# Strassen-type up projection: activations made in two rounds, four products of the first two blocks regrouped, and one weight tile given its own buffer

## The chip, the cores and the metric

The kernel runs on one core of a Trainium2 chip. The metric is the device time of one execution in microseconds (us), the median of several runs. The engines that matter here are TensorE (PE in the profile: matrix products and transposes), VectorE (DVE: sums, differences, evictions), ScalarE (ACT: casts, copies, activations), GpSimd (POOL: a few sums and powers) and SyncE (SP), whose queue issues most of the transfers. Each engine works through its own list in a fixed order; semaphores make it wait for the others.

## The reference

One layer of a transformer over 1024 tokens of width 1024: a modulated norm, a token mixer (retention beside differential attention), an output projection with a gated residual, and then the part that this change touches:

```python
def conv_ffn(h, w_up, conv_w, conv_b, w_down):
    u = h @ w_up
    up = jnp.pad(u, ((0, 0), (1, 1), (0, 0)))
    u = up[:, :-2] * conv_w[0] + up[:, 1:-1] * conv_w[1] + up[:, 2:] * conv_w[2] + conv_b
    a, b = jnp.split(u, 2, axis=-1)
    return (jax.nn.silu(a) * b) @ w_down
...
    x = x + g1 * y_lat
    h2 = rms_norm(x, norm2_g[l]) * (1.0 + sc2) + sh2
    x = x + g2 * conv_ffn(h2, w_up[l], conv_w[l], conv_b[l], w_down[l])
```

`h` is 1024 x 1024, `w_up` is 1024 x 5632 and `w_down` 2816 x 1024; all is in 32-bit floats, and the final norm follows.

## The kernel before

**How a product is made.** Every 32-bit operand is split into a high and a low part (`split_op` for weights, `split_to` for activations: a cast on ACT, then a difference on DVE, lines 894 and 895, 941 and 942). A product then takes three matmuls per slice of 128 rows of the contraction: high by high, high by low, low by high (`passes`, lines 129 to 131). `product` does four slices, so 12 matmuls of 128x128 by 128x512.

**The up projection in blocks.** Block j holds 128 columns of the half `a` of `w_up` and the 128 matching ones of the half `b` (22 blocks). It is computed as a two by two matrix product in Winograd's form of Strassen's method, with 7 products (P1 to P7, 84 matmuls) in place of 8. The weights of a block come as two tiles `wra` and `wrb` of 512 KB, each with two buffers. Each tile holds two halves of the contraction: a1, a2, b1, b2. P1, P2 and P4 take a1, a2 and b2 as they are; P5, P6, P7 and P3 take sums made on POOL by `combined` (lines 1024 to 1027): s1 = b1 + b2, s2 = s1 - a1, s3 = a1 - b1 into `cmb` (three buffers), and a2 - s2 written over b1. The activations come as B11, B21 (first 512 tokens), B22 and the differences T1, T2, T3, T4: P1 uses B11, P2 B21, P3 B22, P4 T4, P5 T1, P6 T2, P7 T3.

**Banks.** P1, P6, P7 and P4 of a block add up in one PSUM bank, `chain`, which is copied out after each of them. P2 has the bank `second`. P5 and then P3 add up in the bank `third`, which is read once after P5 (into `ub`, line 1109) and once after P3 (into `ua`, line 1114). There are eight banks in pools of 4, 2 and 2.

**What surrounds the change.** The output projection ends with the norm of the eight token tiles (`norm2`). The first four tiles are turned beside it into B11 and B21 (`turned0`). The last four are turned by `turned1`, a generator of which `tick` runs a step every so many slices of a product (`beside(turned1(), 0.45, ...)`: 0.45 steps per slice): four rounds, each of which makes the difference for T1, then B22, T2, T3 and T4 for one slice, with 2 transposed groups on PE, 9 DVE and 7 ACT instructions. Beside it PE computes P1 and P2 of the first `NPRE` = 4 blocks, whose weights `pre` were loaded and for three blocks also split (`early`) during the output projection; the fourth split is made here. Then follow the sums of block 0 (`ops0`) and the loop over the blocks (line 1125): load of block j+1, `begin` (P1 and P2, unless done), `end` and `gated` of the block before (P3, P4, then convolution, silu, product and the operands for the down projection), and `middle` (P6, P5, P7).

**What sets the order.** Outside a part of the attention, the order of the instructions on each engine is not the one of the source. A planner puts them in order when the program is built, by the order of the source as priority and by its own estimates of when operands and buffers are ready. What it decided is fixed at run time: an instruction that waits holds up all behind it on its engine. Pools with `reuse_waits="tile"` wait for the tiles whose place they take, others for their whole predecessor.

The weights' split tiles `whi`, `wlo` rotate through six buffers (`wop`), so the split of one product can be made six products ahead of its use at most.

Of the kernel before, what the change touches and what calls it, by code (L numbers as in the profile page):

```python
# [8 lines left out]
F32 = mybir.dt.float32  # L9
# [63 lines left out]
def kernel(  # L73
# [78 lines left out]
    with ExitStack() as p1:  # L152
# [738 lines left out]
    def split_op(src):  # L891
        hi = wop.tile([P, 4, P], F32R, name="whi")
        lo = wop.tile([P, 4, P], F32R, name="wlo")
        nc.scalar.copy(hi, src)  # L894
        nc.vector.tensor_tensor(out=lo, in0=src, in1=r32(hi), op=ALU.subtract)  # L895
        return hi, lo

    def raw_load(name, src):
        o = wst.tile([P, KD, P], F32, name=name)
        nc.sync.dma_start(out=o, in_=src)  # L900
        return o

# [37 lines left out]
    def split_to(src, tt, c):  # L940
        nc.scalar.copy(tt[0][:, c, :], src)  # L941
        nc.vector.tensor_tensor(out=tt[1][:, c, :], in0=src, in1=r32(tt[0][:, c, :]), op=ALU.subtract)
# [4 lines left out]
            split_to(raw0[:, d, :], (B11, B21)[d // 4], d % 4)  # L947
            yield

    NPRE = 4  # L950
    with ExitStack() as p3:
        ps = p3.enter_context(tc.tile_pool(name="ps3", bufs=2, space=PSUM))
        for n in range(2):
            sl = wo_first if n == 0 else []
            for _ in wo_gen if n == 0 else out_weights(n, sl):
                pass
            for t in range(NT):
                pt = ps.tile([P, 512], F32, name="po3", tag="mm")
                for k in range(KD):
                    passes(pt, tuple(yT[a][t // 4][:, k, t % 4 * P : (t % 4 + 1) * P] for a in range(2)), sl[k], k == 0, k == KD - 1)  # L960
                    tick()
                dst = x1[t][:, n * 512 : (n + 1) * 512]
                gated = wo.tile([P, 512], F32, name="gated")
                nc.vector.tensor_tensor(out=gated, in0=pt, in1=g1[:, n * 512 : (n + 1) * 512], op=ALU.mult)
                nc.vector.tensor_tensor(out=dst, in0=gated, in1=dst, op=ALU.add)
                if n == 1:
                    norm2(t)
                    if t == 1:
                        pre = [raw_load("wra" if j < 2 else "wrb", w_up[j]) for j in range(NPRE)]
                        early = [[split_op(a[:, c : c + 4, :]) for c in (0, 4)] for a in pre[:3]]  # L970
                    if t == 3:
                        beside(turned0(), 0.5, -3.0)
        beside(iter(()), 0.0)
# [11 lines left out]
    def turned1():  # L985
        def less(o, a, b):
            nc.vector.tensor_tensor(out=o, in0=a, in1=b, op=ALU.subtract)

        for c in range(4):
            r12 = tmpT.tile([P, 512], F32, name="r12", bufs=2)  # L990
            turned(1, c, r12, True)
            b11, b21 = raw0[:, c, :], raw0[:, c + 4, :]
# [12 lines left out]
            yield  # L1005

    def up_load(j):
        return raw_load("wra", w_up[j]), raw_load("wrb", w_up[j + NF])
# [9 lines left out]

    def combined(j):

        a, b = raws.pop(0)
        a1, a2, b1, b2 = a[:, 0:4, :], a[:, 4:8, :], b[:, 0:4, :], b[:, 4:8, :]
        s1, s2, s3 = [cmb.tile([P, 4, P], F32, name="cmb", bufs=3) for _ in range(3)]
        nc.gpsimd.tensor_tensor(out=s1, in0=b1, in1=b2, op=ALU.add)  # L1024
        nc.gpsimd.tensor_tensor(out=s2, in0=s1, in1=a1, op=ALU.subtract)
# [4 lines left out]
    chain, second, first = {}, {}, {}  # L1030
# [12 lines left out]
    beside(iter(()), 0.0)  # L1043
    raws.append(up_load(1))
    pstS.close()
    tmpS.close()
    rawp.close()
    psC = ctx_r.enter_context(tc.tile_pool(name="psC", bufs=2, space=PSUM, side="right"))
    bank_cycle = itertools.cycle([psC] * 2 + [psB] * 2 + [psA] * 4)


    with ExitStack() as p4:
        up = p4.enter_context(tc.tile_pool(name="up", bufs=2, side="right", reuse_waits="tile"))

        def conv(u, idx):
# [4 lines left out]
            nc.vector.scalar_tensor_tensor(out=t[:, : L - 1], in0=u[:, 1:], scalar=w[2], in1=t[:, : L - 1], op0=ALU.mult, op1=ALU.add)  # L1060
            return t

        held = {}

        def down_operands(j, g):
# [17 lines left out]
        class Block:  # L1083
            def __init__(self, j):
                self.j = j
                self.ops = combined(j) if j else ops0

            def op(self, p):
                return split_op(self.ops[p])
# [10 lines left out]
                self.ub = up.tile([P, L], F32, name="ub")  # L1100

            def middle(self):
                product(self.chain, self.op("p6"), T2, False)
                nc.scalar.copy(self.ua[:, 512:], self.chain)
                self.third = bank("third")
                product(self.third, self.op("p5"), T1, True)
                product(self.chain, self.op("p7"), T3, False)
                nc.scalar.copy(self.ub[:, 512:], self.chain)
                nc.vector.tensor_tensor(out=self.ub[:, 512:], in0=self.third, in1=self.ub[:, 512:], op=ALU.add)

            def end(self):
                product(self.third, self.op("p3"), B22, False)
# [10 lines left out]

        last = None
        for j in range(NF):
            if 2 <= j + 1 < NF:
# [252 lines left out]
```

## Time and profile before

| | us |
|---|---|
| median of three runs | 1448.55 (1448.17 to 1450.31) |
| the profiled execution's own time | 1441.0 |
| its span, first to last instruction | 1439.2 |
| PE busy in the span | 1379.9 (96%) |
| DVE busy | 1003.8 (70%) |
| ACT busy | 732.4 (51%) |
| POOL busy | 340.8 (24%) |
| granted PE clock, mean | 0.992 |
| PE busy, 700 to 783.32 (output projection) | 83.32 of 83.32 |
| PE busy, 783.32 to 866.65 (first blocks) | 75.68 of 83.33 |
| PE busy, 870 to 1215 (further blocks) | 345.00 of 345.00 |

In the profile each instruction has a line number, an operation, and the tiles that it writes and reads; "idle before" is the time its engine stood still ahead of it, with the instruction that ended the wait. Matmuls are pipelined: their start to start distance, not their duration, is their cost on PE.

### The profile page before, as it was taken

Reading aid. Unit: us, or ns where it says so; the run is one execution under the profiler, and the core shown is the slowest. Engines: PE = TensorE matmul, PEld = TensorE weight load, DVE = VectorE, ACT = ScalarE, POOL = GpSimd, SP = SyncE. Lnnn points to the kernel's source line nnn. Section 1 sums busy time; section 2 is a strip of 40 time slices with the busy share of each in tenths; the row PEclk is TensorE's granted clock in tenths of the full one; section 3 lists DMA queues with packets and bytes.
Section 4 is the critical chain, followed back from the end, with each engine's and each line's share of the span. In section 5 each row is a group of like instructions: output and inputs, shape, how many; then the busy total and the mean of one; then the engine's idle time right before and its main releaser. Section 6 shows DMA issues by size and latency. Waiting matters only on the chain.

```text
span 1439.2 us, 19420 instructions
## 1 busy us (share of the span) xinstructions
PE 1379.9 (96%) x6924; PEld 1141.9 (79%) x6924; DVE 1003.8 (70%) x1493; ACT 732.4 (51%) x1394; POOL 340.8 (24%) x451
## 2 busy tenths in 40 slices
PE   6999999999899899999999899999999999999996
PEld 2678787887777789999888677888888888888885
DVE  3565655333677598888346888878777777998457
ACT  3535512322456688998224655555555545455533
POOL 1210000022787323431002253322223230000001
PEclk9999999999999999999999999999999999999999
DMA  8557655466455767480511123223222224953224
GB/s 332 199 194 240 219 196 190 137 193 195 134 173 164 208 156 164 121 143 1 220 62 78 59 104 118 108 110 110 92 87 93 110 110 174 391 206 102 101 95 176
DMA packets 107673, 218.30 MB, mean 152 GB/s; under 512 B 8948, under 2 KB 47348, under 8 KB 106680
## 3 DMA queue, kind: packets, MB, share of 16 engines
q1 hardware_dynamic: 99448, 192.14, 38.3%
q0 software_dynamic: 8128, 24.91, 7.7%
q8 instruction: 55, 0.90, 0.3%
q14 instruction: 42, 0.34, 0.1%
HBM read 159.61 MB, written 57.41 MB: 151 GB/s over the span
## 4 chain that ended last, share of the span: by engine, by line
PE 66%; DVE 8%; DMA 5%; POOL 3%; issue 3%; ACT 3%; SPq 0%; POOLq 0%; DVEq 0%; ACTq 0%
PE chain L129 5%; PE pv L760 5%; PE chain L130 5%; PE pA L728 5%; PE chain L131 5%; PE c L131 4%; PE c L129 4%; PE c L130 4%; PE third L130 2%; PE third L129 2%; PE third L131 2%; DMA W<-w_down 2%; PE pt L748 2%; PE pn L130 2%; PE pn L131 2%
## 5 line engine op out<-in xcount | busy, mean ns | idle before, releaser
L129 PE MATMUL chain<-T,whi 128*128 128x512 f32 x264 | 103.8, 394 | 4.9 <-ACT T L941 3.3
L129 PE MATMUL pl<-hT,whi 128*128 128x512 f32 x256 | 107.1, 419 | 0.0
L130 PE MATMUL chain<-T,whi 128*128 128x512 f32 x264 | 103.2, 391 | 0.0
L131 PE MATMUL chain<-T,wlo 128*128 128x512 f32 x264 | 102.6, 390 | 0.0
L131 PE MATMUL pl<-hT,wlo 128*128 128x512 f32 x256 | 100.5, 393 | 0.0
L130 PE MATMUL pl<-hT,whi 128*128 128x512 f32 x256 | 100.5, 393 | 0.0
L731 DVE TENSOR_REDUCE mt<-pA 128x1 f32<-128x1280 f32 x64 | 95.3, 1490 | 3.3 <-PE pA L728 1.5
L728 PE MATMUL pA<-ks,qhl 128*128 128x512 f32 (+1 forms) x384 | 91.6, 375 | 4.7 <-ACT p L735 4.7
L1024 POOL TENSOR_TENSOR cmb<-wrb 128x512 f32<-128x512 f32 x22 | 36.2, 1647 | 243.2 <-DMA wrb<-w_up 141.3
L131 PE MATMUL c<-whi,ghl 128*128 128x512 f32 x232 | 90.4, 390 | 0.2 <-DVE ghl L1183 0.2
L130 PE MATMUL c<-wlo,ghl 128*128 128x512 f32 x232 | 90.3, 389 | 0.0
L129 PE MATMUL c<-whi,ghl 128*128 128x512 f32 x232 | 90.2, 389 | 0.0
L115 POOL TENSOR_TENSOR sm<-sm,mhalf 128x1 f32<-128x1 f32 x26 | 16.1, 621 | 304.7 <-DVE sm L114 301.4
L735 ACT ACTIVATE p<-pA,mt 128x1280 f32<-128x1280 f32 x64 | 85.5, 1336 | 4.6 <-DVE mt L731 4.5
L894 ACT CAST whi<-cmb 128x512 fp32r<-128x512 f32 x66 | 41.0, 622 | 83.5 <-PE chain L130 63.7
L728 PEld LDWEIGHTS pA<-ks,qhl 128*128 128x128 f32 x384 | 68.9, 193 | 17.5 <-ACT p L735 5.8
L129 PE MATMUL pn<-whi,hT 128*128 128x512 f32 x192 | 79.1, 412 | 0.0
L760 PE MATMUL pv<-va,aT 128*128 128x128 f32 x640 | 77.0, 275 | 0.1
L131 PE MATMUL pn<-whi,hT 128*128 128x512 f32 x192 | 75.9, 398 | 0.5 <-DVE hT L540 0.5
L130 PE MATMUL pn<-wlo,hT 128*128 128x512 f32 x192 | 76.1, 396 | 0.0
L895 DVE TENSOR_TENSOR wlo<-cmb,whi 128x512 fp32r<-128x512 f32 x66 | 60.7, 922 | 20.2 <-ACT whi L894 20.2
L760 PEld LDWEIGHTS pv<-va,aT 128*128 128x128 f32 x640 | 74.0, 192 | 0.7 <-DVE yT L789 0.3
(301 smaller groups left out, 3884.1 us busy)
## 6 DMA issues: line engine op xcount, KB each, us to landing
wm<-w_mod SPq DMA_DIRECT2D x32, 512.0 KB, 4.4
raw<-w_in SPq DMA_DIRECT2D x28, 512.0 KB, 4.4
wra<-w_up SPq DMA_DIRECT2D x24, 512.0 KB, 3.2
wrb<-w_up SPq DMA_DIRECT2D x24, 512.0 KB, 3.5
W<-w_down SPq DMA_DIRECT2D x44, 256.0 KB, 6.4
ad<-s SPq DMA_DIRECT2D x20, 512.0 KB, 3.4
wra<-ad SPq DMA_DIRECT2D x20, 512.0 KB, 3.2
wrb<-ad SPq DMA_DIRECT2D x18, 512.0 KB, 3.3
```

The source lines that it names most:

```text
L115: nc.gpsimd.tensor_tensor(out=out_ap, in0=out_ap, in1=mhalf[:, :n], op=ALU.pow)
L129: mm(ps, lh, rh, start=first, stop=False, skip_group_check=more)
L130: mm(ps, lh, rl, start=False, stop=False, skip_group_check=more)
L131: mm(ps, ll, rh, start=False, stop=last, skip_group_check=more)
L728: mm(self.pa[m][:, c0:c1], self.q[:, i, m, qs], self.k[:, m, c0:c1], start=(i == 0), stop=(i == 1))
L731: nc.vector.tensor_reduce(out=self.mt[:, m : m + 1], in_=self.pa[m][:, :LK], axis=AX.X, op=ALU.min)
L735: nc.scalar.activation(self.p[m], self.pa[m][:, :LK], AF.Exp, scale=-1.0, bias=self.mt[:, m : m + 1], accum_out=self.s[:, m : m + 1])
L748: nc.tensor.transpose(self.pt[g][:, i, :], self.p[0][:, (4 * g + i) * P : (4 * g + i + 1) * P], ident)
L760: mm(self.pv, self.aT[:, c, :], self.v[:, c, :], start=(c == 0), stop=(c == NKT - 1))
L894: nc.scalar.copy(hi, src)
L895: nc.vector.tensor_tensor(out=lo, in0=src, in1=r32(hi), op=ALU.subtract)
L1024: nc.gpsimd.tensor_tensor(out=s1, in0=b1, in1=b2, op=ALU.add)
```

## The change

- **Loads.** `NPRE` goes from 4 to 3. The freed buffer of `wrb` and the next ones of `wra` take the weights of blocks 0 and 1 (`NSUM` = 2), all four tiles loaded during the output projection. The weights of block 2 are asked for at the start of the block loop, its b tile first, into a pool of its own (`third_b`), then its a tile, in this order on the queue. The loads of blocks 3 and later follow in the loop as before.
- **Sums.** For blocks 0 and 1 POOL makes three of the four sums in place, over the loaded tiles, during the output projection (`sums_in_place`); the fourth, s3 = b2 - a1, which is the same value, goes to `cmb` afterwards.
- **Two rounds.** `turned1` first makes T1, B22 and T3 for all four slices, with the value that T2 needs left in place in `raw0`; a second round of four steps makes T2 and T4. The rate is 0.36 steps per slice.
- **Products ahead.** P5 and P3 of blocks 0 and 1 are split and computed straight after P1 and P2 of the first three blocks, each in its own bank (`fifth`, `third`), ahead of P6. In these two blocks `middle` adds `fifth` to `ua` and to `ub`, `end` adds `third` to `ua`.

The core of the diff:

```diff
-    NPRE = 4
+    NPRE = 3
+    NSUM = 2
+    def up_load(j):
+        if j == NSUM:
+            start = len(nc.cur_bb.bb.instructions)
+            b = raw_load("wrb", w_up[j + NF], third_b)
+            a = raw_load("wra", w_up[j])
+            in_order(start)
+            return a, b
+        return raw_load("wra", w_up[j]), raw_load("wrb", w_up[j + NF])
+
+    def sums_in_place(a, b):
+        a1, a2, b1, b2 = a[:, 0:4, :], a[:, 4:8, :], b[:, 0:4, :], b[:, 4:8, :]
+        nc.gpsimd.tensor_tensor(out=b1, in0=b1, in1=b2, op=ALU.add)
+        nc.gpsimd.tensor_tensor(out=a1, in0=b1, in1=a1, op=ALU.subtract)
+        nc.gpsimd.tensor_tensor(out=a2, in0=a2, in1=a1, op=ALU.subtract)
...
+                        raws = [up_load(j) for j in range(NSUM)]
+                        for a, b in raws:
+                            sums_in_place(a, b)
...
-            less(r22, r22, b11)
-            split_to(r22, T2, c)
+            less(b11, r22, b11)
             split_to(r12, T3, c)
-            less(b21, b21, r22)
+            yield
+        for c in range(4):
+            b11, b21 = raw0[:, c, :], raw0[:, c + 4, :]
+            split_to(b11, T2, c)
+            less(b21, b21, b11)
             split_to(b21, T4, c)
             yield
...
+        if j < NSUM:
+            s3 = cmb.tile([P, 4, P], F32, name="cmb", bufs=3)
+            nc.gpsimd.tensor_tensor(out=s3, in0=b2, in1=a1, op=ALU.subtract)
+            return dict(p3=a2, p4=b2, p5=b1, p6=a1, p7=s3)
...
-    beside(turned1(), 0.45, 0.0)
+    ops = [combined(j) for j in range(NSUM)]
+    split_ahead = []
+    beside(turned1(), 0.36, 0.0)
     for j in range(NPRE):
-        if j == 3:
-            early.append([split_op(pre[j][:, c : c + 4, :]) for c in (0, 4)])
...
         if j < 2:
+            split_ahead += [split_op(ops[i][("p5", "p3")[j]]) for i in range(NSUM)]
             first[j] = first_sum(chain[j], second[j])
-    raws = [up_load(0)]
-    ops0 = combined(0)
+    pstS.close()
+    psC = ctx_r.enter_context(tc.tile_pool(name="psC", bufs=2, space=PSUM, side="right"))
+    for j, pool in enumerate((psA, psC)):
+        fifth[j] = bank("fifth", pool)
+        product(fifth[j], split_ahead[j], T1, True)
+    for j, pool in enumerate((psB, psC)):
+        third[j] = bank("third", pool)
+        product(third[j], split_ahead[NSUM + j], B22, True)
...
+        third_b = p4.enter_context(tc.tile_pool(name="third_b", bufs=1, side="right", reuse_waits="tile"))
+        raws.append(up_load(NSUM))
...
+                if j < NSUM:
+                    self.third, self.fifth = third[j], fifth[j]
+                    nc.vector.tensor_tensor(out=self.ua[:, 512:], in0=self.fifth, in1=self.ua[:, 512:], op=ALU.add)
+                else:
+                    self.third = self.fifth = bank("third")
+                    product(self.third, self.op("p5"), T1, True)
```

More of the change, by code (lines that the diff above doesn't have):

```diff
@@ L896, in split_op, with raw_load @@
         return hi, lo
-    def raw_load(name, src):
-        o = wst.tile([P, KD, P], F32, name=name)
+    def raw_load(name, src, pool=None):
+        o = (pool or wst).tile([P, KD, P], F32, name=name)
         nc.sync.dma_start(out=o, in_=src)
@@ L969 @@
                         pre = [raw_load("wra" if j < 2 else "wrb", w_up[j]) for j in range(NPRE)]
-                        early = [[split_op(a[:, c : c + 4, :]) for c in (0, 4)] for a in pre[:3]]
+                        early = [[split_op(a[:, c : c + 4, :]) for c in (0, 4)] for a in pre]
+                        raws = [up_load(j) for j in range(NSUM)]
+                        for a, b in raws:
+                            sums_in_place(a, b)
                     if t == 3:
@@ L1028, in combined @@
         return dict(p1=a1, p2=a2, p3=b1, p4=b2, p5=s1, p6=s2, p7=s3)
-    chain, second, first = {}, {}, {}
-    beside(turned1(), 0.45, 0.0)
+    chain, second, first, fifth, third = {}, {}, {}, {}, {}
+    ops = [combined(j) for j in range(NSUM)]
+    split_ahead = []
+    beside(turned1(), 0.36, 0.0)
     for j in range(NPRE):
-        if j == 3:
-            early.append([split_op(pre[j][:, c : c + 4, :]) for c in (0, 4)])
         chain[j] = bank("chain", psA)
@@ L1085, in __init__ @@
                 self.j = j
-                self.ops = combined(j) if j else ops0
+                self.ops = ops[j] if j < NSUM else combined(j)
             def op(self, p):
@@ L1102, in middle @@
             def middle(self):
+                j = self.j
                 product(self.chain, self.op("p6"), T2, False)
                 nc.scalar.copy(self.ua[:, 512:], self.chain)
-                self.third = bank("third")
-                product(self.third, self.op("p5"), T1, True)
+                if j < NSUM:
[4 more added lines that the diff above has]
+                    product(self.third, self.op("p5"), T1, True)
                 product(self.chain, self.op("p7"), T3, False)
                 nc.scalar.copy(self.ub[:, 512:], self.chain)
-                nc.vector.tensor_tensor(out=self.ub[:, 512:], in0=self.third, in1=self.ub[:, 512:], op=ALU.add)
+                nc.vector.tensor_tensor(out=self.ub[:, 512:], in0=self.fifth, in1=self.ub[:, 512:], op=ALU.add)
             def end(self):
-                product(self.third, self.op("p3"), B22, False)
+                if self.j >= NSUM:
+                    product(self.third, self.op("p3"), B22, False)
                 product(self.chain, self.op("p4"), T4, False)
@@ L1125 @@
         for j in range(NF):
-            if 2 <= j + 1 < NF:
+            if NSUM < j + 1 < NF:
                 raws.append(up_load(j + 1))
```

7 lines of the change are left out of this document (1 added, 6 removed).

## The prediction

> **What bounds the kernel now.** I read first the busy time by stage, then who waited for whom on PE where it isn't full, then PE's timeline around each wait, and last the chain that ended the longest one.
>
> ```profile
> core 0: us, PE busy (x) PEld busy (x) DVE busy (x) ACT busy (x) POOL busy (x), PEclk, DMA share, GB/s
> 700.00:783.32 83.32, 83.32 (x384) 68.99 (x383) 41.91 (x68) 23.83 (x39) 5.11 (x8) 1.00 0.33 127
> 783.32:866.65 83.33, 75.68 (x333) 59.49 (x331) 72.43 (x90) 48.54 (x77) 36.23 (x20) 0.98 0.23 85
> 870.00:1215.00 345.00, 345.00 (x1523) 285.50 (x1522) 275.49 (x311) 175.88 (x254) 93.60 (x69) 1.00 0.29 106
> 818.36:821.51 3.15, 3.15 (x7) 2.48 (x8) 3.15 (x4) 1.70 (x4) 1.65 (x2) 0.50 0.00 0
> ```
>
> PE is full on both sides of the stretch from 783.32 to 866.65, and the change moves only work of that stretch (plus POOL sums into the stage before it). The number of matmuls stays the same. So the change is worth what becomes of PE's lost time in these 83.33 us.
>
> ```profile
> 783.32 0.39 PE L129 MATMUL chain<-yT,whi 128*128 128x512 f32 x1
> ...
> 794.98 0.66 PE L934 MATMUL pt<-ident,x 128*128 128x128 f32 x4 [0.94 <-ACT r L936]
> ...
> 804.92 0.39 PE L129 MATMUL chain<-yT,whi 128*128 128x512 f32 x1
> ...
> 810.36 0.39 PE L129 MATMUL chain<-T,whi 128*128 128x512 f32 x1
> ...
> 814.64 0.39 PE L129 MATMUL third<-yT,whi 128*128 128x512 f32 x1
> 818.36 0.80 PE L129 MATMUL chain<-T,whi 128*128 128x512 f32 x1 [3.33 <-ACT T L941]
> ...
> 837.43 0.39 PE L131 MATMUL chain<-T,wlo 128*128 128x512 f32 x1
> 838.48 0.50 PE L129 MATMUL chain<-T,whi 128*128 128x512 f32 x1 [0.67 <-ACT ua L1015]
> 840.43 0.39 PE L131 MATMUL chain<-T,wlo 128*128 128x512 f32 x1
> 841.72 0.50 PE L129 MATMUL third<-yT,whi 128*128 128x512 f32 x1 [0.90 <-DVE ub L1109]
> 855.13 0.40 PE L131 MATMUL chain<-T,wlo 128*128 128x512 f32 x1
> 856.36 0.50 PE L129 MATMUL third<-yT,whi 128*128 128x512 f32 x1 [0.83 <-DVE ub L1109]
> 865.33 0.39 PE L131 MATMUL third<-yT,wlo 128*128 128x512 f32 x1
> 866.65 0.50 PE L129 MATMUL chain<-T,whi 128*128 128x512 f32 x1 [0.93 <-ACT ua L1104]
> ```
>
> From 804.92 to 810.36 are the 24 matmuls of the last P1 and P2, so one costs 0.227 us start to start. A distance between starts less 0.227 is a loss. At 818.36 it is 3.49; then the window of clock 0.50 holds 7 matmuls in 3.15 us, a loss of about 1.5; at 838.48, 841.72, 856.36 and 866.65 it is 0.82, 1.06, 1.00 and 1.09, and about 0.1 more for the slower matmul behind each: 4.4 together; at 794.98 the wait is 0.9. Sum 10.3 us. As a check, 300 matmuls lie between 783.32 and 866.65 by the source (96, 60 for each of three blocks, 24 of the fourth): 68.1 us, and eight transposed groups at some 0.45; 83.33 less 71.7 leaves 11.6. So about 11 us, 0.8%, is all there is to win.
>
> The chain shows why the largest wait arose.
>
> ```profile
> 810.68 5.13 POOL cmb L1024
> 815.81 0.07 issue
> 815.88 1.27 POOL cmb L1025
> 817.15 0.02 issue
> 817.17 0.62 ACT whi L894
> 817.79 0.53 ACT T L941
> 818.32 0.04 issue
> 818.36 0.80 PE chain L129
> ```
>
> ACT's fixed order put a cast of block 1's P6 weights in front of the last casts for T. That cast waited for a POOL sum, which took 5.13 us beside a DVE that was never idle; DVE and PE then stood still for lack of T.
>
> **The change part by part.**
>
> ```profile
> 827.84 1.29 POOL L1024 TENSOR_TENSOR cmb<-wrb 128x512 f32<-128x512 f32 x1 [4.76 <-DMA wrb<-w_up]
> 787.77 1.63 DVE L929 TENSOR_SCALAR x<-x,sm 128x1024 f32<-128x1024 f32 x1
> 791.03 1.77 DVE L987 TENSOR_TENSOR raw<-r,raw 128x512 f32<-128x512 f32 x1
> 792.90 0.69 DVE L987 TENSOR_TENSOR r<-r,r 128x512 f32<-128x512 f32 x1
> ...
> 813.98 0.69 DVE L987 TENSOR_TENSOR raw<-raw,r 128x512 f32<-128x512 f32 x1
> ```
>
> *Loads and sums moved forward.* Six POOL sums of some 1.3 us, 8 us, go into the output projection, where the first fence has POOL busy for 5.11 of 83.32 us and DVE for 41.91: nothing on the path. If that cover were gone, 8 us of POOL would push the norm's powers (POOL's work there), and PE with them. The loads are 512 KB each as before; no queue gains a transfer, one (block 1's b) moves ahead. Of the eight POOL sums of blocks 0 and 1 only the two for s3 stay behind 783, before DVE fills up. So POOL's 5.13 us, and ACT's wait for it, have no successor there: a gain of 3.49 + 1.5 = 5.0, if the products ahead find their operands. It also spares DVE the waits beside POOL: the difference at 791.03 took 1.77, that at 792.90 took 0.69, so a meeting costs 1.1, and the scaling at 787.77, which the last transposes need, I take to have lost 0.9 of its 1.63 in the same way. `turned1` then starts on DVE at 790.1 in place of 791.03.
>
> *Products ahead, two rounds.* PE reaches P5 of block 0 at 783.32 + 72 x 0.227 + 8 x 0.45 = 803.2, and its fourth slice, which needs the last of T1, at 805.3. DVE in a closed row takes 0.602 each (35 starts from 792.90 to 813.98). Ahead of T1's last low half stand 20 of the first round, 2 of `first_sum` and 4 splits of P5 and P3: 26, that is 15.7, to 805.8. A wait of 0.5. PE reaches P6 of block 0 at 803.2 + 0.5 + 48 x 0.227 = 814.6, its fourth slice at 816.6. T2's last is DVE's 42nd (30, 10 of the second round, 2 splits): 815.4. No wait, but I add 0.5 for order and semaphores. Added: 1.0. Bounds: nothing, or what the second rival costs. Without these 48 matmuls PE would stand at P6 from 803.7 on, as T2 comes no sooner: that is what they cover. `NPRE` of 3 only puts 24 matmuls back behind P7 of block 2.
>
> *The wait of the transposes* at 794.98 (0.9) falls at a rate of 0.36 steps in place of 0.45, and without the two splits of the fourth block in ACT's way: I take half, 0.5; bounds 0 and 0.9.
>
> *Blocks 0 and 1.* They now have three products, 8.2 us of PE, while DVE has one instruction more in each (0.6, in the account below).
>
> ```profile
> L1060 DVE SCALAR_TENSOR_TENSOR tconv<-ub,cl,tconv 128x1023 f32<-128x1023 f32 x3 | 3.8, 1274 | 0.0
> ```
>
> P3 has its own bank, so the waits of P3 for `ub` (841.72, 856.36) go in blocks 0 and 1, and in block 2 24 matmuls (P1, P2 of block 3) come between. In their place stands P5 of block 2, at 815.1 + 7 x 12 x 0.227 = 834.2, whose bank is that of block 1's `fifth` and is free after `ub` of block 1. DVE until then, from 815.4: 15 short ones (two of T4, six splits, six additions, one sum of block 2's) 9.0, four convolution steps of 1.27, 5.1, a product of the same size 1.3 and a difference 0.6, and 1.1 for each of the four POOL sums of block 2: 20.4, to 835.8. A wait of 1.6. With 0.3 for others, 1.9 of the 4.4 stay: a gain of 2.5. Bounds 0 and 4.4 of gain, or the third rival's loss.
>
> *Third block's loads.*
>
> ```profile
> 823.69 0.33 SPq L900 DMA_DIRECT2D wrb<-w_up x1
> ```
>
> Block 2's b takes the place of `r12`, free after DVE's 30th, 808.2, so it is there by 812.4 (4.1 from the issue to its first use at 827.84, above). The a tile, behind it on SP, waits for P6(0)'s split and is there by 820 at the latest; two POOL sums, one of them at the chain's 5.13 and one at 1.3, end by 827; PE wants P6(2) at 831.5. Hidden, with 4 us in hand; on SP nothing else is queued behind but the stores of the blocks.
>
> The Trainium skill's page "SBUF — State Buffer", section "Who interferes with whom", says that when a DVE instruction with two inputs in SBUF meets a GpSimd one that reads SBUF, the later one blocks until the earlier has finished. By it POOL would get in behind one DVE instruction, and the 5.13 us disagrees: POOL stayed out until DVE paused; 791.03 agrees. By the page, block 2's first sum would hold up T2's end by 1.1, and the sum would be 1442.6 us; by the row it is as follows.
>
> **The sum.** -5.0 - 2.5 - 0.5 + 1.0 = -7.0. The profiled execution took 1441.0 (span 1439.2 and 1.8 around it), so it would become 1434.0; the median of the runs shown, 1448.55, is 0.5% above that execution, and I carry the same 7.0 over: 1441.5.
>
> **The rivals.**
> 1. *All waits go*: -10.3, 1438.2. For it: the accounts above miss T1 by 0.5 and the bank by 1.6 only. Against: four waits of some 1 us have different causes.
> 2. *The idle moves in front of P5, and the change loses.* If the planner puts the second round and the splits of P6 and P7 ahead of the last of T1 on DVE, that one comes at 815.4; 39 matmuls (8.9) remain until P6, which starts at 824.9, and a wait that long brings the slow clock again (1.5): -7.0 + 9.8 + 1.5 = +4.3, 1452.8. It decides from about 811 on, that is nine DVE instructions out of order. For it: the chain above, in which a cast of a later product stood ahead of T's. Against: the source has T1's part first, and the planner goes by the source among what is ready.
> 3. *DVE bounds blocks 0 and 1.* DVE's list of 20.4 us stands against 19 us of PE. If the order puts the convolution of block 1 and a delayed POOL sum ahead of `ub` (3 conv steps and 2 waits), P5 of block 2 waits 6 us more: -1.0, 1447.5, no difference.
> 4. *The moved loads do nothing by themselves.* The chain above has no transfer in it; then only the sums and the order count, and the forecast stands.
>
> **How the numbers follow.** A measurement of this kernel tells about 0.2%, 2.9 us, from no change. Forecast 0.50, rival 1 0.17, a part of the gain over 2.9 us 0.05: faster 0.72. Rival 3: same 0.10. Rival 2: slower 0.18. The range goes from rival 1 with 0.7 to spare, 1437.5, past rival 3 to 1450.0, and leaves out most of rival 2.
>
> **What would show it.** Right: no POOL sum of L1024's kind between 790 and 810; PE without a wait over 1 us up to P6 and no window of clock 0.50; P6 of block 0 near 815 after 120 matmuls; P1 of block 3 near 842. Wrong: PE idle at the first `fifth` or `third` on T or B22; a wait of P5 of block 2 on `ub`; ACT waiting on a POOL sum with a cast that PE needs behind it.

## The result and the profile after

The changed kernel takes 1442.21 us (median of 22 runs, 1437.82 to 1447.09) against 1446.34 us for the kernel before, run beside it. The ratio is 0.997, 95% interval 0.9958 to 0.9981, so about 4.3 us less (2.7 to 6.1). The forecast was a gain of 7.0, to 1441.5: the sign was right, the size was not, and that the time itself comes out close is luck: the kernel before took 1446.34 here and not the 1448.55 that the forecast started from.

The two profiled executions stand 1.1 us apart already at the first matmul of P1, so I measure a distance inside the execution: from the first matmul of P1 of block 0 to the first matmul of the down projection. Before it is 783.32 to 1212.23, 428.91 us; after it is 784.46 to 1209.40, 424.94 us. That is 3.97 less and fits the ratio. (Where an expectation below says 425.2, it counts to the second matmul of the down projection.)

The busy time by stage of the changed kernel, columns as in the prediction: the output projection, the stretch of the change, the further blocks, and a piece of slow clock.

```profile
700.00:784.46 84.46, 84.46 (x389) 69.95 (x388) 43.27 (x68) 23.88 (x39) 13.07 (x13) 1.00 0.35 130
784.46:866.68 82.22, 77.37 (x346) 62.27 (x345) 76.12 (x98) 50.32 (x80) 23.18 (x15) 0.98 0.25 87
870.00:1210.00 340.00, 340.00 (x1502) 281.53 (x1501) 268.11 (x304) 174.48 (x252) 90.92 (x68) 1.00 0.29 103
862.20:866.70 4.50, 4.50 (x13) 3.54 (x14) 3.84 (x5) 1.07 (x3) 0.00 (x0) 0.62 0.41 130
```

In the output projection POOL is busy for 13.07 us where it was 5.11, and PE stays full: the sums moved there at no cost. PE in the stretch still loses 4.85 us outright (82.22 less 77.37), and there is a slow clock again, only elsewhere. PE's timeline shows where.

```profile
784.46 0.39 PE L129 MATMUL chain<-yT,whi 128*128 128x512 f32 x1
...
804.62 0.40 PE L129 MATMUL fifth<-yT,whi 128*128 128x512 f32 x1
...
810.19 0.39 PE L129 MATMUL third<-yT,whi 128*128 128x512 f32 x1
...
815.63 0.39 PE L129 MATMUL chain<-T,whi 128*128 128x512 f32 x1
...
824.29 0.50 PE L129 MATMUL chain<-T,whi 128*128 128x512 f32 x1 [0.92 <-ACT ub L1144]
...
829.86 0.50 PE L129 MATMUL chain<-T,whi 128*128 128x512 f32 x1 [1.86 <-ACT ua L1136]
...
862.20 0.50 PE L129 MATMUL chain<-T,whi 128*128 128x512 f32 x1 [2.08 <-ACT ua L1136]
```

Up to P6 of block 0 at 815.63 PE never waits: 24 matmuls of P5 between 804.62 and 810.19 and 24 of P3 up to 815.63, at 0.23 each. The old wait for T of 3.49 is gone. But three new waits stand behind it, at P4 of block 0 (1.07 by start to start distance less 0.227), P7 of block 1 (2.02) and P7 of block 3 (2.23), and the last is followed by some eight matmuls at 0.43, another 1.6. All three wait for a copy of a bank by ACT. ACT's timeline shows what stood ahead of these copies.

```profile
823.13 0.62 ACT L894 CAST whi<-cmb 128x512 fp32r<-128x512 f32 x1 [0.98 <-POOL cmb L1050]
823.66 0.58 ACT L1144 COPY ub<-chain 128x512 f32<-128x512 f32 x1
...
826.49 1.28 ACT L1157 ACT_TABLE_LOAD   x1 [1.73 <-DVE tconv L1089]
827.79 1.06 ACT L1157 ACTIVATE tconv<-tconv 128x1024 f32<-128x1024 f32 x1
828.75 0.57 ACT L1152 COPY ub<-chain 128x512 f32<-128x512 f32 x1
829.22 0.59 ACT L1136 COPY ua<-chain 128x512 f32<-128x512 f32 x1
...
860.62 1.06 ACT L1157 ACTIVATE tconv<-tconv 128x1024 f32<-128x1024 f32 x1 [1.61 <-DVE tconv L1089]
861.58 0.57 ACT L1136 COPY ua<-chain 128x512 f32<-128x512 f32 x1
```

The copy for P4 of block 0 stands behind a cast that waited for a POOL sum of block 2. The copy for P7 of block 1 stands behind the silu of block 0 (L1157), which waits for the convolution on DVE and then loads its table. The copy for P7 of block 3 stands behind the silu of block 2, although P5 still lies between P6 and P7 there; in the kernel before, ACT had this copy first (at 866.04, the silu at 867.02). Why that sum and that convolution are late shows on POOL, on SP and on DVE, in this order.

```profile
714.12 1.65 POOL L964 TENSOR_TENSOR wrb<-wrb 128x512 f32<-128x512 f32 x1 [17.74 <-DMA wrb<-w_up]
...
820.23 1.30 POOL L1049 TENSOR_TENSOR cmb<-wrb 128x512 f32<-128x512 f32 x1 [30.83 <-DMA wrb<-w_up]
821.81 1.29 POOL L1050 TENSOR_TENSOR cmb<-cmb,wra 128x512 f32<-128x512 f32 x1 [0.28 <-DMA wra<-w_up]
```

```profile
816.53 0.33 SPq L900 DMA_DIRECT2D wrb<-w_up  x1
```

```profile
815.77 0.70 DVE L942 TENSOR_TENSOR T<-raw,T 128x512 fp32r<-128x512 f32 x1
...
822.18 2.00 DVE L1088 SCALAR_TENSOR_TENSOR tconv<-ua,cl,tconv 128x1023 f32<-128x1023 f32 x1 [1.38 <-ACT tconv L1087]
...
824.88 1.53 DVE L1089 SCALAR_TENSOR_TENSOR tconv<-ua,cl,tconv 128x1023 f32<-128x1023 f32 x1
```

Block 2's b is asked for at 816.53, right after DVE's last split for T4 (815.77): its place overlaps the end of `raw0`, not only `r12`. So its first POOL sum starts at 820.23, not in the low 810s, and the sums meet DVE's convolution, whose two steps take 2.00 and 1.53, where one that meets no POOL sum takes 1.27. (That is no loss against before: there the first step of block 0 met a sum too, and the two took 2.31 and 1.27.)

### The profile page after: what moved, and what is told of

It reads as the page before. It is cut to its first block, busy times and chain, and to the rows that moved or that the text cites. A ratio compares the mean times of both kernels' runs of the same rounds, so it can differ in the third digit from the quotient of the medians.

```text
span 1436.0 us, 19423 instructions
## 1 busy us (share of the span) xinstructions
PE 1378.6 (96%) x6924; PEld 1142.0 (80%) x6924; DVE 1001.1 (70%) x1495; ACT 732.8 (51%) x1394; POOL 335.3 (23%) x451
## 4 chain that ended last, share of the span: by engine, by line
PE 69%; DVE 8%; DMA 3%; issue 3%; POOL 3%; ACT 3%; POOLq 0%; SPq 0%; DVEq 0%; ACTq 0%
PE chain L129 5%; PE chain L131 5%; PE chain L130 5%; PE pv L760 5%; PE pA L728 5%; PE c L131 4%; PE c L130 4%; PE c L129 4%; PE third L131 2%; PE third L129 2%; PE third L130 2%; PE pt L748 2%; PE pn L130 2%; PE pn L131 2%; PE pn L129 2%
## 5 line engine op out<-in xcount | busy, mean ns | idle before, releaser
L1049 POOL TENSOR_TENSOR cmb<-wrb 128x512 f32<-128x512 f32 x20 | 26.8, 1339 | 249.8 <-DMA wrb<-w_up 144.6
L894 ACT CAST whi<-wra 128x512 fp32r<-128x512 f32 x55 | 33.8, 624 | 83.6 <-PE third L130 42.3
```

## The experiments

Each is an edit of the changed kernel, except the last, which edits the kernel before. "Distance" is that of the section above, before 428.91, changed 424.94.

**1. Products ahead undone.** P5 and P3 of blocks 0 and 1 go back into the blocks; early sums and two rounds stay.

```diff
-            split_ahead += [split_op(ops[i][("p5", "p3")[j]]) for i in range(NSUM)]
...
-                if j < NSUM:
-                    self.third, self.fifth = third[j], fifth[j]
...
-                else:
-                    self.third = self.fifth = bank("third")
-                    product(self.third, self.op("p5"), T1, True)
+                self.third = self.fifth = bank("third")
+                product(self.third, self.op("p5"), T1, True)
```

> P5 and P3 of blocks 0 and 1 go back behind P6 and P7; loads, sums in place and the two rounds stay. I look at the stretch from the first P1 to the first P1 of block 4 (86.2 us before, 82.2 in the changed kernel). Theory (the products ahead cover the making of T2, and in exchange no longer cover the copies of the bank between P6, P7 and P4): PE stands still for 5 to 8 us on T2 at some 805 to 815, with the slow clock behind it, and the two waits for ua and ub copies in blocks 0 and 1 (1.1 and 2.0) shrink; sum 85 to 88 us, ratio to the kernel before 0.998 to 1.001. Rival (only POOL's sums moved forward count, the products ahead are worth nothing): the stretch stays at 82 us or gets shorter by the two waits, 80, ratio 0.996 or below.

Measured: 1442.14 us, ratio 0.9973 (0.9959 to 0.9988), stretch 82.17, distance 424.89: the changed kernel's numbers, as the rival had it. But PE's timeline of this run has other waits.

```profile
813.06 0.50 PE L130 MATMUL chain<-T,whi 128*128 128x512 f32 x1 [0.85 <-DVE T L942]
...
814.80 0.80 PE L129 MATMUL chain<-T,whi 128*128 128x512 f32 x1 [1.01 <-ACT ua L1129]
...
836.71 0.50 PE L129 MATMUL third<-yT,whi 128*128 128x512 f32 x1 [1.72 <-DVE ub L1134]
```

PE now waits for T2, as the prediction said it would without these matmuls, but for 1.0 us and not for the 11.7 of its account (803.7 to 815.4): the planner put P5 of block 0 between the slices of P6. PE also pays a slow clock behind the second wait. In return the waits at P4 of block 0 and at P7 of blocks 1 and 3 are gone. In the orders that the planner chose, moving P5 and P3 is a trade at par. What exactly removed the waits at P7 this run doesn't tell: P5 is back as a cover, but the planner also has the silus of blocks 0 and 1 behind the copies again (silu at 831.07 after the copy at 828.10, 844.90 after 843.79).

**2. One round.** T2 and T4 are made in the first round again; the products stay ahead.

```diff
-            less(b11, r22, b11)
+            less(r22, r22, b11)
+            split_to(r22, T2, c)
             split_to(r12, T3, c)
-            yield
-        for c in range(4):
-            b11, b21 = raw0[:, c, :], raw0[:, c + 4, :]
-            split_to(b11, T2, c)
-            less(b21, b21, b11)
+            b21 = raw0[:, c + 4, :]
+            less(b21, b21, r22)
```

> T2 and T4 are made in the first round again, slice by slice with T1; all else is as in the changed kernel. Theory (T1's last low half must be DVE's 26th, not its 38th): PE waits some 6 to 8 us for T1 in the fourth slice of the first P5, with the slow clock behind it (1.5), and none of it comes back, since P6 stands behind P5 and P3 in PE's order: stretch 89 to 92 us, ratio to the kernel before 1.002 to 1.004. Rival (the order of the two rounds does not matter since DVE's sum of work is the same and P6 waits less for T2): stretch 82 to 84 us, ratio 0.997 to 0.998.

Measured: 1445.32 us, ratio 0.9996 (0.9982 to 1.001), stretch 83.84, distance 426.56. Worse than the changed kernel, but by less than expected, and the stretch is the rival's. PE comes to the fourth slice of the first P5 4.2 us before T1 is there, but the planner put eleven matmuls of P3 and P6 into that gap, so that 1.33 of waiting remains; another 1.0 sits in a longer wait of P7 of block 1 (3.26 from start to start against 2.25), and the wait at P4 of block 0 is gone.

```profile
817.63 0.50 PE L130 MATMUL fifth<-yT,whi 128*128 128x512 f32 x1 [1.16 <-DVE yT L942]
...
838.04 0.50 PE L129 MATMUL chain<-T,whi 128*128 128x512 f32 x1 [2.87 <-ACT ua L1134]
```

**3. Both undone, so that only the early loads and sums stay.** The diffs of 1 and 2 together.

> Of the change only the loads and the sums of blocks 0 and 1 in place, the three blocks ahead and the third block's tile stay; P5 and P3 are back in the loop and T2, T4 back in the one round. Mark: from the first P1 to P2 of block 4 (88.9 us before, 84.9 in the changed kernel, 84.9 with the products back alone). Theory (the gain comes from block 1's sums being out of ACT's and DVE's way, and not from the products ahead or the rounds): mark 84 to 86 us, ratio to the kernel before 0.996 to 0.998. Rival (the two rounds carry it, since T1 is early enough to feed P5 while T2 is made): mark 87 us or more, ratio 0.999 or above.

Measured: 1442.97 us, ratio 0.9981 (0.997 to 0.9993), mark 87.66, distance 427.66: the mark is the rival's, the ratio lies between the two. The wait for T is there again, but smaller than the 3.33 of before.

```profile
813.96 0.50 PE L129 MATMUL chain<-T,whi 128*128 128x512 f32 x1 [1.53 <-ACT T L941]
```

The four distances together:

| us | one round | two rounds |
|---|---|---|
| P5, P3 in the blocks | 427.66 | 424.89 |
| P5, P3 ahead | 426.56 | 424.94 |

By these profiles the early sums are worth 1.25 of the 3.97, the second round 1.6 to 2.8, and the products ahead something only beside a single round. By the runs' times the two kernels of one round can't be told apart (their intervals overlap), so the order within that column stays open. And each distance is that of a single execution: experiment 4 has the changed kernel's waits and is 1.62 longer by one more piece of slow clock, so a difference of that size in this table isn't firm.

**4. The sums written later in the source.** The three in-place sums are moved behind the norm in the source.

```diff
-                        for a, b in raws:
-                            sums_in_place(a, b)
...
+    for a, b in raws:
+        sums_in_place(a, b)
     for j in range(NPRE):
```

> The six sums of blocks 0 and 1 in place come after the norm stage instead of beside the output projection; all else is as in the changed kernel. Theory (POOL beside a full DVE was the cause of the wait at 818 before): POOL's sums start at about 783, each costs DVE 1.1 us or waits for a pause of DVE, the splits of P5 and P3 come late, and PE waits 4 to 8 us at P5 or P3: stretch 87 to 91 us, ratio 1.000 to 1.004. Rival (the sums have room before DVE fills up at 791, so moving them was worth nothing): stretch 82 to 83.5 us, ratio 0.997.

Measured: 1442.11 us, ratio 0.9969 (0.9956 to 0.9983), distance 426.56. It told nothing: the order written out put the sums where they had been on POOL, at the same place in the output projection, and the same three waits stand in PE's timeline (the longer distance is a second piece of slow clock, behind the wait of P7 of block 1). The next experiment does it properly.

**5. The sums held on POOL behind the last power of the norm.**

```diff
+    with tc.issue_after(pows[-1].ins):
+        for a, b in raws:
+            sums_in_place(a, b)
```

> The six sums in place are held on POOL behind the last power of the norm, by an order of their own (moved in the source alone, in the run before, they kept their early place). Theory (POOL's sums beside a full DVE cost): eight POOL sums run from about 788 to 803 beside turned1, each costs DVE 1.1 us or waits; P5 of blocks 0 and 1 and P3 find their splits late, PE waits 4 us or more ahead of P6; mark 88 to 92 us, ratio to the kernel before 1.000 to 1.004. Rival (they fit in ahead of the time at which DVE is full): mark 85 us, ratio 0.997.

Measured: 1449.02 us, ratio 1.0026 (1.0011 to 1.0041), mark 92.99, distance 432.99, 8 us worse than the changed kernel. PE's and POOL's timelines of this run:

```profile
799.07 0.44 PE L936 MATMUL pt<-ident,x 128*128 128x128 f32 x2 [1.89 <-DVE x L931]
...
805.50 0.66 PE L936 MATMUL pt<-ident,x 128*128 128x128 f32 x4 [1.11 <-ACT r L938]
...
809.65 0.66 PE L936 MATMUL pt<-ident,x 128*128 128x128 f32 x4 [1.43 <-ACT r L938]
```

```profile
794.26 2.54 POOL L966 TENSOR_TENSOR wrb<-wrb 128x512 f32<-128x512 f32 x2
796.76 3.41 POOL L967 TENSOR_TENSOR wra<-wrb,wra 128x512 f32<-128x512 f32 x2
```

Late sums lie beside the norm's scaling and the differences on DVE, and the transposes wait three times, 4.4 us together; P5 then waits twice for T1, 1.0 together, and P6 doesn't wait. With sums this late the rest of the change is a loss.

**6. Another place for block 2's b.** The small tile `sm2` is allocated ahead of `raw0`, so that `third_b` no longer overlaps `raw0`.

```diff
-    raw0 = rwp.tile([P, KD, 512], F32, name="raw0")
     sm2 = rwp.tile([P, 64], F32, name="sm2")
+    raw0 = rwp.tile([P, KD, 512], F32, name="raw0")
```

> One small tile is allocated ahead of raw0, so that the third block's b tile no longer takes a corner of raw0's place and need not wait for the last T4 split (its load was issued at 816.5 in the changed kernel, the a tile right behind it). Theory (late loads of block 2 hold up the POOL sum, and the cast that waits for it holds up the ub copy on ACT): b is asked for at about 809, a at about 816.0, the sum s2 is done about 1 us earlier, the wait of P4 of block 0 falls from 1.1 to 0.3 or less: stretch 81.4 us. Rival (P4's wait is the plain exposure of the copy after P7, since P5 no longer lies between): the wait stays near 1, stretch 82.2 us. In both the ratio is within 0.996 to 0.998.

Measured: 1443.45 us, ratio 0.9986 (0.9971 to 1.0001), stretch 83.76, distance 426.48. The b tile is asked for at 811.11, 24.3 us after the first P1 in place of 32.1, and P4 of block 0 no longer waits. But the first POOL sum then falls beside a DVE that is never idle (8.40 of 8.44 us busy with 15 instructions), and P7 of block 1 waits 1.25 longer. POOL, the busy time of that stretch, the last two DVE instructions in it, and PE:

```profile
814.52 8.44 POOL L1049 TENSOR_TENSOR cmb<-wrb 128x512 f32<-128x512 f32 x1 [22.80 <-DMA wrb<-w_up]
```

```profile
814.52:822.96 8.44, 8.44 (x38) 6.84 (x38) 8.40 (x15) 3.01 (x5) 8.44 (x1) 1.00 0.35 104
```

```profile
821.73 0.68 DVE L1139 TENSOR_TENSOR ua<-fifth,ua 128x512 f32<-128x512 f32 x1
822.44 0.69 DVE L1151 TENSOR_TENSOR ua<-third,ua 128x512 f32<-128x512 f32 x1
```

```profile
832.35 0.80 PE L129 MATMUL chain<-T,whi 128*128 128x512 f32 x1 [3.12 <-ACT ua L1136]
```

An earlier load bought a longer sum: it starts 8.0 us earlier, counted from the first P1, and ends 0.9 earlier. What P4 of block 0 gains comes back at P7 of block 1, whose copy stands behind the silu as in the changed kernel and starts no earlier (44.9 us after the first P1, there 44.8), and the longer wait brings a second piece of slow clock. The Trainium skill's page "SBUF — State Buffer", section "Who interferes with whom", has the later of two such instructions wait until the earlier one has finished; this trace disagrees, as the 5.13 us of before did: POOL stayed out over a dozen DVE instructions, up to the two shown, which read a bank. (The 1442.6 that the prediction worked out from the page had block 2's first sum hold up T2; in the changed kernel that sum came after T2 and met it nowhere.)

**7. The silu behind the next block's copy.** On ACT the silu of blocks 0 to 2 is issued after the copy of the next block's P6.

```diff
-                nc.scalar.copy(self.ua[:, 512:], self.chain)
+                self.copied = nc.scalar.copy(self.ua[:, 512:], self.chain)
...
-                nc.scalar.activation(ta, ta, AF.Silu)
+                with tc.issue_after(after.copied.ins) if after else nullcontext():
+                    nc.scalar.activation(ta, ta, AF.Silu)
...
-                last.gated()
+                if j > NPRE:
+                    last.gated()
...
+            if last is not None and j <= NPRE:
+                last.gated(blk)
```

> In blocks 0 to 2 the silu on ACT is put behind the next block's copy of P6 out of the bank; all else is as in the changed kernel. Theory (P7 of block 1 and of block 3 wait because this copy stands on ACT behind a silu, which waits for DVE's convolution, and in block 0 behind a table load as well): the waits of 2.25 and 2.46 us with the slow clock behind them fall to 0.5 at most; mark 84.9 less 1.8 less 4.0, 79 to 80.5 us, ratio to the kernel before 0.993 to 0.995. Rival (DVE's list is the bound of these blocks, ACT only passes its wait on): waits of the same length stand elsewhere, on ub, ua or a split, mark 84 us or more, ratio 0.997.

Measured: 1435.87 us (6 runs), ratio 0.9929 (0.9914 to 0.9944), mark 80.15, distance 420.41, as the theory said. The view of who waited for whom on PE, over the whole stretch of this run, shrinks to two lines (total, times, longest):

```profile
PE chain L129 <- ACT ub L1144: 0.9, 1, 0.9
PE chain L129 <- ACT ua L1136: 0.8, 1, 0.8
```

So the order on ACT, with the silus of blocks 0 and 2 ahead of the copies, cost the changed kernel 4.5 us. DVE's list isn't the bound: the convolution step that the first silu waits for ends 42 us after the first P1 in both runs, and it holds up PE only where that silu stands ahead of a copy. This version beats both kernels. It wasn't tried with the products back in the blocks.

**8. The table loaded early.** A dummy silu of one column into a new tile, before the blocks.

```diff
+    tload = kp.tile([P, 1], F32, name="tload")
...
+    nc.scalar.activation(tload, r32(T4[0][:, 3, 0:1]), AF.Silu)
```

> One silu on a single column, result unused, stands behind the last T4 cast on ACT, so that the table load of 1.28 us comes in ACT's pause at 816 to 818 and not at 826.5. Theory (the table load lies in the chain of block 1's wait): the wait of P7 of block 1 falls from 2.25 to about 1.0, that of block 3 stays at 2.4; mark 83.7 us, give or take 1.7 for the slow clock, ratio 0.996. Rival (the load is hidden beside DVE's convolution, the copy waits for something else): the wait stays above 2, mark 84.9.

Measured: 1451.85 us, ratio 1.0031 (1.0018 to 1.0044), distance 434.48. The wait of P7 of block 1 is gone (the 0.52 shown is for another copy, that of P1 of block 2 in `first_sum`, L1036 here), yet the kernel is slower than before: in the further blocks, where nothing was changed, each matmul takes longer. PE's timeline and the further blocks of this run:

```profile
829.33 0.51 PE L130 MATMUL chain<-T,whi 128*128 128x512 f32 x1 [0.52 <-ACT ua L1036]
```

```profile
870.00:1210.00 340.00, 340.00 (x1459) 273.08 (x1458) 262.07 (x295) 168.19 (x243) 88.96 (x67) 1.00 0.28 101
```

1459 matmuls in 340 us against 1502: 0.2330 each in place of 0.2264, PE full and its clock at 1.00 in both. Suspect: the new tile moves the addresses of all tiles behind it. Two runs test it.

**9. The dummy silu without the new tile.** Its result goes into a padding tile that exists.

```diff
-    pad(kp, 96)
+    unused = pad(kp, 96)
...
+    nc.scalar.activation(unused[:, 0:1], r32(T4[0][:, 3, 0:1]), AF.Silu)
```

> The table load ahead again, by a dummy silu, but its result goes into a tile that the kernel has anyway, so that no address moves. Leaves nothing of the computation out. Theory (in e7 the shift of the addresses by a new tile made blocks 4 to 21 slower, not the table load): the window 870 to 1210 us holds some 1500 matmuls as in the changed kernel, not 1459; the wait of P7 of block 1 on the copy of ua falls from 1.86 to about 0.9, from the first P1 to the first down-projection product it takes about 424, the ratio is about 0.996. Rival (the dummy silu, or the table load's new place, slows the blocks): some 1460 matmuls, about 434, ratio 1.003.

Measured: 1440.12 us, ratio 0.9962 (0.9946 to 0.9977), distance 424.34. The further blocks and PE's waits of this run:

```profile
870.00:1210.00 340.00, 340.00 (x1502) 281.63 (x1501) 269.03 (x305) 174.27 (x251) 90.29 (x68) 1.00 0.29 103
```

```profile
829.09 0.50 PE L131 MATMUL chain<-T,whi 128*128 128x512 f32 x1 [0.57 <-ACT ua L1037]
...
862.09 0.50 PE L131 MATMUL chain<-T,whi 128*128 128x512 f32 x1 [2.67 <-ACT ua L1139]
```

The spacing is back. In place of the 1.86 at P7 of block 1 PE waits 0.57 for the copy of P1 of block 2 (L1037 here), so the table load as such is worth 1.3 there, of which P7 of block 3 takes 0.6 back.

**10. Only the addresses.** The changed kernel with 128 bytes of padding in place of 96; its instructions are the same and, but for a few on DVE, in the same order.

```diff
-    pad(kp, 96)
+    pad(kp, 128)
```

> The changed kernel with an unused tile of 128 bytes where it has one of 96, so that the tiles behind it lie 32 bytes further on; instructions and, but for a few on DVE, their order are the same. Theory (addresses alone set the spacing of the matmuls): the window 870 to 1210 us holds some 1460 matmuls in place of 1502, from the first P1 to the first down-projection product it takes 433 to 436 in place of 425.2, ratio 1.003. Rival (addresses do nothing): 1502, 425.2, 0.997 as the changed kernel.

Measured: 1452.67 us, ratio 1.0049 (1.0033 to 1.0066), distance 435.19. The further blocks of this run:

```profile
870.00:1210.00 340.00, 340.00 (x1458) 273.07 (x1458) 261.67 (x296) 167.89 (x243) 91.62 (x68) 1.00 0.29 103
```

Addresses alone cost 10 us here, more than the whole change is worth. The changed kernel itself stands on the good side, with the same 1502 matmuls as before.

**11. The silu behind and b's other place, together** (the diffs of 7 and 6).

> The silu of blocks 0 to 2 behind the next block's copy (e6) and the third block's b tile in a place that does not wait for raw0 (e4), both together. Theory (the copy of ub for P4 of block 0 waited behind a cast that waited for block 2's late loads, and with the silu out of the way nothing takes its place): the wait of P4 of block 0 falls from 1.34 to 0.5 or less, the mark of P2 of block 4 is at 79 to 79.5, first P1 to first down-projection product 419 to 420, ratio 0.992. Rival (as in e4 the wait only moves to the next product): mark 80.2, 420.4, ratio 0.993.

Measured: 1436.24 us (6 runs), ratio 0.9924 (0.9901 to 0.9948), distance 419.45. Of PE's waits in the stretch only two small ones are left:

```profile
831.48 0.50 PE L129 MATMUL chain<-T,whi 128*128 128x512 f32 x1 [0.41 <-ACT ua L1035]
...
832.97 0.50 PE L129 MATMUL chain<-T,whi 128*128 128x512 f32 x1 [0.29 <-ACT ua L1136]
```

With the silu out of the way the wait did not move on, as it had in 6; but the 0.96 us in the trace are less than the runs' times can tell (the interval overlaps that of 7).

**12. The silu behind, in the kernel before** (the edit of 7 alone).

> The kernel before with only the silu of blocks 0 to 2 put behind the next block's copy. Theory (the silu on ACT mattered for the changed kernel because P5 and P3 no longer covered the copies; in the kernel before two of its waits, at 838.48 and 866.65, are on the copy of ua, 0.82 and 1.09): at most these go, first P1 to first down-projection product 427 to 428 in place of 428.9, ratio 0.9985. Rival (the order on ACT is a cost of its own in any version): as much as in the changed kernel, -4.8, 424, ratio 0.9965.

Measured: 1444.28 us, ratio 0.9991 (0.9977 to 1.0005), distance 429.02: nothing. The two waits on `ua` of this run stand as before:

```profile
843.49 0.50 PE L129 MATMUL chain<-T,whi 128*128 128x512 f32 x1 [0.66 <-ACT ua L1015]
...
871.64 0.50 PE L129 MATMUL chain<-T,whi 128*128 128x512 f32 x1 [0.93 <-ACT ua L1104]
```

Neither expectation held, and the run doesn't test them, because the edit changed nothing in these blocks: in the kernel before, the planner had the silus of blocks 0 to 2 behind the copies of P6 already. ACT of the kernel before, then of this run, shows it for block 0 (copy of P6 of block 1, silu of block 0, copy of P1 of block 2):

```profile
833.93 0.57 ACT L1104 COPY ua<-chain 128x512 f32<-128x512 f32 x1
...
836.89 1.06 ACT L1120 ACTIVATE tconv<-tconv 128x1024 f32<-128x1024 f32 x1
837.86 0.57 ACT L1015 COPY ua<-chain 128x512 f32<-128x512 f32 x1
```

```profile
838.93 0.57 ACT L1104 COPY ua<-chain 128x512 f32<-128x512 f32 x1
...
841.90 1.06 ACT L1121 ACTIVATE tconv<-tconv 128x1024 f32<-128x1024 f32 x1
842.87 0.57 ACT L1015 COPY ua<-chain 128x512 f32<-128x512 f32 x1
```

The third line is the copy that PE waits for at 838.48 (here 843.49): P1 of block 2 was computed by 802, and DVE is done with the `ua` of block 0, whose buffer the copy takes, at 836.3; from there on the copy stands behind the silu. The copy for the wait at 866.65 stood behind two other activations (L1058). So ACT's order cost PE something in the kernel before too; whether the silu ahead of the copies of P6 would have cost as much there wasn't tried.

## Why the prediction was partly right

The sum was -5.0 - 2.5 - 0.5 + 1.0 = -7.0. By the trace it is as follows.

- *Sums early and the wait for T, -5.0:* right in size, for the three parts of the change together. The wait at T is gone, no POOL sum runs between 790 and 820, and P6 of block 0 starts 31.2 us after the first P1 (forecast 31.8). The early sums alone don't remove it: in experiment 3 they cut the wait from 3.33 to 1.53 and the distance by 1.25. The second round or the products as a cover, each added alone, leave a wait of 1.0 for T2 (experiment 1) or 1.3 for T1 (experiment 2). Experiment 5 shows that late sums cost 8 us, but mostly at the transposes. POOL's sums beside the output projection cost nothing there, as said.
- *The wait of the transposes, -0.5:* more, -1.4, outside its bounds of 0 and 0.9. The same 72 matmuls and eight transposed groups took 21.60 before (783.32 to 804.92) and 20.16 after (784.46 to 804.62).
- *Products ahead, two rounds, +1.0:* 0. P5 met no wait for T1 and P6 none for T2. DVE's last split for the second round's T4 starts at 815.77, near the account, which has T4 right behind 815.4. But that PE would stand at P6 from 803.7 to 815.4 without these products is not what experiment 1 shows: there it waits 1.0 for T2.
- *Blocks 0 and 1, -2.5:* this step failed, by its sign. The four later waits of 4.4 were to shrink to 1.9; in their place came three of 1.07, 2.02 and 2.23, with 1.6 of slow clock and some 0.3 of slower matmuls behind: 7.2, a loss of 2.8. The account was of DVE and its bank alone and had P5 of block 2 waiting 1.6 for `ub`. That wait doesn't exist. What was left out is ACT and its order: a cast stood ahead of the copy for P4 of block 0, a silu with its table load of 1.28 ahead of that for P7 of block 1, a silu ahead of that for P7 of block 3. Experiment 7 shows it: moving the silus alone gives back 4.5. In blocks 0 and 1 the copy has also lost P5 as a cover; in block 3 P5 is in its place, and what differs from before is that the planner put the silu of block 2 ahead of the copy. How much the lost cover costs by itself no run tells (experiment 1 changed the order as well, experiment 12 changed nothing), and why the planner changed the order stays open.
- *Third block's loads, hidden with 4 us in hand:* wrong. The b tile was asked for 7 us later, counted from the first P1, than the 808.2 of the account, because its place overlaps `raw0` as well (in experiment 6, without the overlap, it is within 0.6 of the account), and the 1.07 at P4 of block 0 is its price. Yet the earlier place of experiment 6 gained nothing by itself. In the prediction's own account one POOL sum was to take 5.13 beside DVE; there it took 8.44.

-5.0 - 1.4 + 2.8 is -3.6; the distance shrank by 3.97, and the 0.4 between them is in small gaps that I did not assign. Of the rivals, the second did not occur: nine DVE instructions out of order would have shown at `fifth` or `third`. The third had the place of the loss, blocks 0 and 1, and nearly its size (6.0 against the forecast, measured 5.3), but named DVE's list and `ub` where it was the order on ACT. (In the second rival's sum 815.4 and 8.9 make 824.3, not 824.9, so it stood 0.6 too high; this decides nothing.) The first is what experiments 7 and 11 come near to: 10.3 us were to be won, and the distance of 11 is 9.5 below that of before.

## What to carry to other kernels

When work is moved forward to cover one wait, ask what it covered where it stood: list for each engine what then lies between a bank's last matmul and the copy that frees it, the in-order queue of ACT included. Instructions that nobody waits for soon, such as an activation at the end of a block, belong behind the copies that PE waits for; where a planner sets the order, read in the trace what it chose, before the change and after, and that an edit meant to move an instruction did move it. And before a few tenths of a per cent are put down to an edit, compare the matmul spacing in a stretch that the edit doesn't touch.

## What the runs showed of the hardware

- A shift of tiles by 32 bytes of padding made every matmul of the up projection's further blocks 3% slower (340 us over 1458 in place of 1502, their mean duration 395 ns in place of 389), at a granted clock of 1.00. The down projection was not slower: in its 220 us there are 944 matmuls, in the changed kernel 938. Which operand's address does it wasn't tried.
- A slow clock followed distances of 2.2 to 2.5 us between starts and not only the 3.7 of before: in the changed kernel that of 2.46 at 862.20 has it and that of 2.25 at 829.86 has not, in experiment 10 one of 2.21 has it. The length alone doesn't decide: in experiment 1 it followed two of 1.24 and 1.41 within 2 us (at 814.80), in experiment 2 one of 3.26 has it not (at 838.04). The Trainium skill's page "TensorE: Matmul & The Clock Gate", section "What's actually happening", has the clock fall after an idle window of some 3.4 us that runs freely; the waits here are shorter, so this trace does not agree with it as a bound. Either way a wait near 2 us can cost 1.6 us more than its length.
- A POOL sum of 1.3 us beside a DVE that is never idle took 5.13 us before and 8.44 us in experiment 6. Before, it ended 1.1 us after DVE paused (814.67); in experiment 6 it ended while DVE was still busy, 1.2 us after DVE began the first of two additions that read a bank (821.73). So a load that comes 8 us earlier brought its sum less than 1 us earlier.
